# The low parts of the stick-breaking keys in both halves of the partitions

## The chip, the cores and the metric

The kernel runs on one core of one Trainium2 chip. A core has TensorE (in the profile PE for matmuls, PEld for its weight loads), VectorE (DVE), ScalarE (ACT), GpSimd (POOL) and a queue for transfers (SP). What counts is the time of one execution on the device in microseconds (us), as the median of several runs.

## The reference

The kernel computes two layers of a decoder trunk over 512 positions of width 1024. Layer 0 mixes with sliding-window attention and, beside it, stick-breaking attention of 8 heads with 64 channels; both layers end in cross-attention and a feed-forward network. Only the stick-breaking part is touched:

```
z = einsum('bqhd,bkhd->bhqk', q[:, t0:t1], k[:, :t1]) * (HEAD_DIM ** -0.5)
log_fail = where(causal, -softplus(z), 0.0)
log_after = cumsum(log_fail, axis=3, reverse=True) - log_fail
a = where(causal, exp(log_sigmoid(z) + log_after), 0.0)
out = einsum('bhqk,bkhd->bqhd', a, v[:, :t1])
```

Blocks of 128 queries see the keys up to their own block, so the four blocks of a head have scores of 128 x 128, 128 x 256, 128 x 384 and 128 x 512.

## The kernel before

All large products run as three matmuls on numbers that are split into a high part, rounded to the matmul's input format, and a low part, the rest: high by high, high by low, low by high (`mm3`, lines 182 to 184). They write the PSUM tile ps_pj, of which there are three buffers.

`sb_pair` handles two heads of 64 channels, which lie in the two halves of the 128 partitions of a query tile qb and a key tile kb_. For head `a`, `hr` is its own half and `orow` the other one. Three tiles are made of 128 x 512: `qs` holds the high part of the queries in `hr` (line 787, ScalarE) and their low part in `orow` (788, VectorE); `ks` holds the high part of the keys in `hr` (789, ScalarE) and the same numbers again in `orow` (790, ScalarE); `kl` holds the low part of the keys in `hr` alone (791, VectorE). The profile calls them sbqs, sbks and sbkl. Each has one buffer per `a`, so the next pair of heads writes where this one read.

For each block n the scores take two matmuls into ps_at (two buffers): line 798 over all 128 rows gives high queries by high keys plus low queries by high keys, line 799 over the 64 rows of `hr` adds high queries by low keys. There are 8 heads of 4 blocks, so 32 of each, 8 of each width. Two sigmoids follow on ScalarE (801, 804), which free the ps_at buffer, a masking of the diagonal on GpSimd (806, 808), a running product and a product on VectorE (811, 813), transposes on TensorE (821), a copy out by ScalarE (823) and the matmuls with the values (829), which use 64 columns of the array and write ps_ov.

Four calls of `sb_pair` are interleaved with work that is independent of them: the output projection of the sliding-window part (`out_proj`, with 512 columns), the preparation of the memory (`mem_prep`: transposes at line 332 into ps_pj, evacuated at 336 and 337) and the projection of the memory to keys and values (`mem_kv`, with 256 columns). Each weight tile is loaded, cast by ScalarE (170) and subtracted by VectorE (171). No order is written out by hand: a scheduler places all instructions by its own estimates of time, and each engine then runs its instructions strictly in the order it was given.

Of the kernel before, what the change touches and what calls it, by code (L numbers as in the profile page):

```python
# [33 lines left out]
def trunk(ctx, tc, x, mem, positions, norm_mix, norm_cross, norm_mem, norm_ffn,  # L34
# [5 lines left out]
    V, G, A, T, SY = nc.vector, nc.gpsimd, nc.scalar, nc.tensor, nc.sync  # L40
# [7 lines left out]
    def tl(pool, shape, tag, bufs=1, dt=FP32):  # L48
        return pool.tile(shape, dt, name=tag, tag=tag, bufs=bufs)
# [8 lines left out]
    def ps(tag, *shape):  # L58
        t = psp.tile([P, 512], FP32, name="ps_" + tag, tag="ps_" + tag, bufs=PSB[tag])
        if not shape:  # L60
            return t
        if len(shape) == 2:
            return t.rearrange("p (a b) -> p a b", b=shape[-1])[:, :shape[0]]
        return t[:, :shape[0]]

    def behind(ins, other):

        tc.add_manual_dep(ins.ins if hasattr(ins, "ins") else ins, (other.ins if hasattr(other, "ins") else other).name,
                          mybir.DependencyInfo(mybir.DependencyClass.NoSync, mybir.DependencyReason.DATA),
                          reason="side by side")  # L70

    def f32(ap):
        return ap.bitcast(FP32)
# [134 lines left out]
    def split(src, hi, lo, eng=None):  # L208
        A.copy(out=hi, in_=src)  # L209
        V.tensor_tensor(out=lo, in0=src, in1=f32(hi), op=ALU.subtract)  # L210
# [299 lines left out]
    def mixer0():  # L510
# [160 lines left out]
        for a in range(2):  # L671
            for g in range(2):
# [4 lines left out]
                             in_=sq.rearrange("p (t h d) -> p t h d", t=2, d=64), axis=AX.X)  # L677
# [101 lines left out]
        def sb_pair(c, qb, kb_):  # L779
            o = ps("ov")  # L780
            ats = []
            for a in range(2):
                hr = slice(64 * a, 64 * a + 64)

                orow = slice(64 - 64 * a, 128 - 64 * a)
                qs, ks, kl = (tl(bp, [P, S], f"{nm}{a}", 1, FP32R) for nm in ("sbqs", "sbks", "sbkl"))
                A.copy(out=qs[hr], in_=qb[hr])
                V.tensor_tensor(out=qs[orow], in0=qb[hr], in1=f32(qs[hr]), op=ALU.subtract)
                A.copy(out=ks[hr], in_=kb_[hr])
                A.copy(out=ks[orow], in_=f32(ks[hr]))  # L790
                V.tensor_tensor(out=kl[hr], in0=kb_[hr], in1=f32(ks[hr]), op=ALU.subtract)
                at = []
                ats.append(at)
                for n in range(NT):
                    wdt = (n + 1) * P
                    z = ps("at")
                    nq = slice(n * P, wdt)
                    T.matmul(z[:, :wdt], lhsT=qs[:, nq], rhs=ks[:, :wdt], start=True, stop=False)
                    T.matmul(z[:, :wdt], lhsT=qs[hr, nq], rhs=kl[hr, :wdt], start=False, stop=True)  # L799
                    be = tl(bp, [P, wdt], f"be{n}", 3 if n < 2 else 2)  # L800
                    A.activation(out=be[:, :wdt], in_=z[:, :wdt], func=AF.Sigmoid)
                    sn_ = tl(bp, [P, S + 1], "sbs", 2)
                    G.memset(sn_[:, wdt:wdt + 1], 1.0)
                    A.activation(out=sn_[:, :wdt], in_=z[:, :wdt], func=AF.Sigmoid, scale=-1.0)
                    dgs = slice(n * P, wdt)
                    G.affine_select(out=sn_[:, dgs], in_=sn_[:, dgs], pattern=[[-1, P]], compare_op=ALU.is_gt,
                                    fill=1.0, base=0, channel_multiplier=1)
                    G.affine_select(out=be[:, dgs], in_=be[:, dgs], pattern=[[-1, P]], compare_op=ALU.is_gt,
                                    fill=0.0, base=0, channel_multiplier=1)
                    ex_ = tl(bp, [P, S], "sbe", 2)  # L810
                    V.tensor_tensor_scan(out=ex_[:, wdt - 1::-1], data0=sn_[:, wdt:0:-1], data1=sn_[:, wdt:0:-1],
                                         initial=1.0, op0=ALU.mult, op1=ALU.bypass)
                    V.tensor_tensor(out=be[:, :wdt], in0=be[:, :wdt], in1=ex_[:, :wdt], op=ALU.mult)
                    at.append(be)

            for kb in range(NT):
                aTs = []
                for a in range(2):
                    pt = ps("tr", NT, P)
                    for n in range(kb, NT):  # L820
                        T.transpose(out=pt[:, n], in_=ats[a][n][:, kb * P:(kb + 1) * P], identity=ident)  # L821
                    aT = tl(bp, [P, NT, P], "sbaT", 2)
                    A.copy(out=aT[:, kb:], in_=pt[:, kb:])
                    aTs.append(aT)

                with tc.high_priority():
                    for a in (1, 0):
                        h = 2 * c + a
                        mm = T.matmul(o[64 * a:64 * a + 64, kb * P:], lhsT=vb[h // 4][:, kb, 64 * (h % 4):64 * (h % 4) + 64],  # L829
                                      rhs=aTs[a][:, kb:].rearrange("p a b -> p (a b)"), start=kb == 0, stop=kb == NT - 1)  # L830
                        if a:
                            first = mm
                        else:
                            behind(mm, first)
            hi, lo = tl(obp, [P, S], f"oh{c}", 1, FP32R), tl(obp, [P, S], f"ol{c}", 1, FP32R)
            split(o, hi, lo)
            oh[4 + c], ol[4 + c] = hi, lo
# [16 lines left out]

        qk_proj(0)
        sb_pair(0, *qks[0])
        sb_pair(1, *qks[1])
        qk_proj(1)
        sb_pair(2, *qks[2])
        sb_pair(3, *qks[3])  # L860

# [269 lines left out]
```

## Time and profile before

| | us |
|---|---|
| median of 3 runs | 1627.89 |
| lowest and highest | 1626.36, 1630.06 |
| the profiled execution | 1628.36 |
| its span, first to last instruction | 1626.6 |
| stick-breaking heads within it | about 150 to 278 |

The profile lists for each engine what it ran and when. A matmul's duration overlaps the next one's, so what a matmul costs in a dense stream is the distance between two starts. A weight load (PEld) of the next matmul can run beside the matmul before it. Idle time before an instruction is put down to what ended it.

### The profile page before, as it was taken

The page shows a single profiled execution, that of the slowest core. Times are in us where ns is not written, and L with a number is a line of the kernel's source. Part 1 is how long each engine was busy: PE and PEld are TensorE (multiplying, and loading weights), DVE is VectorE, ACT ScalarE, POOL GpSimd, SP SyncE. Part 2 cuts the span into 40 slices and gives each one's busy share as a digit, 9 for nine tenths or more (in the row PEclk, how much of TensorE's full clock was granted, in tenths as well). Part 3 has the DMA queues.
Part 4 walks back from the last instruction along what each step waited for, and adds up shares of the span by engine and source line. Part 5 has one row for each costly group of instructions (what it writes and reads, how often), then busy time and mean ns, then how long its engine had stood idle before and what let it go on. Part 6 is the DMA issues. An engine that isn't in the chain of part 4 may idle for free.

```text
span 1626.6 us, 21049 instructions
## 1 busy us (share of the span) xinstructions
PE 1604.9 (99%) x8298; PEld 1332.4 (82%) x8298; DVE 1017.4 (63%) x1662; ACT 706.7 (43%) x1246; POOL 200.9 (12%) x307
## 2 busy tenths in 40 slices
PE   7999999999999999999999999999999999999998
PEld 7987786888788888888789888998888788888887
DVE  6765785666675476366776677655555763674563
ACT  5565675554342243144434344443444441442341
POOL 4301332201100000000422123101002000000000
PEclk9999899999999999999999999999999999999999
DMA  6211331321323223222322222342203323323222
GB/s 191 79 53 63 111 102 61 111 78 52 103 78 104 91 90 104 80 95 74 114 79 59 75 76 78 126 159 79 78 27 104 104 78 104 98 83 104 86 76 72
DMA packets 144479, 145.57 MB, mean 89 GB/s; under 512 B 2844, under 2 KB 143837, under 8 KB 144381
## 3 DMA queue, kind: packets, MB, share of 16 engines
q1 hardware_dynamic: 143882, 143.98, 27.7%
q8 instruction: 66, 1.08, 0.3%
q0 software_dynamic: 96, 0.07, 0.1%
q14 instruction: 32, 0.26, 0.1%
q10 hardware_dynamic: 403, 0.18, 0.0%
HBM read 142.12 MB, written 2.10 MB: 89 GB/s over the span
## 4 chain that ended last, share of the span: by engine, by line
PE 97%; DVE 1%; ACT 1%; DMA 1%; issue 0%; SPq 0%; POOL 0%; DVEq 0%
PE ps_pj L182 28%; PE ps_pj L184 28%; PE ps_pj L183 28%; PE ps_at L953 1%; PE ps_ov L829 1%; PE ps_at L799 1%; DMA sbqk<-in_x_dram 1%; PE ps_tr L821 1%; PE ps_at L182 1%; PE ps_at L184 1%; PE ps_at L183 1%; PE ps_ov L985 0%; PE ps_at L933 0%; PE ps_tr L448 0%; PE ps_ov L750 0%; PE ps_ov L183 0%
## 5 line engine op out<-in xcount | busy, mean ns | idle before, releaser
L183 PE MATMUL ps_pj<-xl,whi 128*128 128x512 f32 x1088 | 432.4, 397 | 0.0
L182 PE MATMUL ps_pj<-xh,whi 128*128 128x512 f32 x1024 | 405.4, 397 | 2.0 <-DVE hF L1004 1.3
L184 PE MATMUL ps_pj<-xh,wlo 128*128 128x512 f32 x1024 | 407.2, 398 | 0.0
L170 ACT CAST whi<-wraw 128x1024 fp32r<-128x1024 f32 (+2 forms) x276 | 264.3, 1006 | 301.1 <-PE ps_pj L183 249.9
L171 DVE TENSOR_TENSOR wlo<-wraw,whi 128x1024 fp32r<-128x1024 f32 (+2 forms) x276 | 320.8, 1197 | 42.4 <-ACT whi L170 41.4
L183 PEld LDWEIGHTS ps_pj<-xl,whi 128*128 128x128 f32 x1088 | 204.4, 188 | 48.2 <-issue 0.7
L182 PEld LDWEIGHTS ps_pj<-xh,whi 128*128 128x128 f32 x1024 | 192.4, 188 | 47.5 <-DVE hF L1004 1.9
L184 PEld LDWEIGHTS ps_pj<-xh,wlo 128*128 128x128 f32 x1024 | 192.4, 188 | 45.4 <-issue 1.0
L281 DVE TENSOR_TENSOR xT<-ps_pj,xT 128x512 f32<-128x512 f32 x80 | 53.7, 687 | 152.5 <-PE ps_pj L184 152.5
L183 PE MATMUL ps_pj<-hid,whi 128*128 128x512 f32 x352 | 138.0, 397 | 0.0
L184 PE MATMUL ps_pj<-hid,wlo 128*128 128x512 f32 x352 | 137.8, 397 | 0.0
L182 PE MATMUL ps_pj<-hid,whi 128*128 128x512 f32 x352 | 137.3, 397 | 0.0
L184 PE MATMUL ps_pj<-whi,xl 128*128 128x256 f32 x416 | 120.1, 291 | 1.5 <-DVE xl L232 1.4
L472 DVE TENSOR_TENSOR fu<-ps_pj,rb 128x512 f32<-128x512 f32 x88 | 60.5, 692 | 90.1 <-PE ps_pj L184 90.0
L242 POOL TENSOR_TENSOR nacc<-nacc,nsq 128x512 f32<-128x512 f32 x36 | 52.5, 1457 | 507.1 <-ACT nsq L241 503.6
L183 PE MATMUL ps_pj<-ol,whi 128*128 128x512 f32 x256 | 101.8, 398 | 0.0
L184 PE MATMUL ps_pj<-oh,wlo 128*128 128x512 f32 x256 | 101.5, 398 | 0.0
L182 PE MATMUL ps_pj<-oh,whi 128*128 128x512 f32 x256 | 99.9, 403 | 1.1 <-ACT oh L209 1.1
L474 ACT ACTIVATE fa<-fu,ccol 128x512 f32<-128x512 f32 x88 | 71.3, 814 | 59.3 <-DVE fu L472 59.3
L182 PE MATMUL ps_pj<-whi,xh 128*128 128x256 f32 x288 | 82.4, 288 | 0.2 <-ACT xh L231 0.2
L183 PE MATMUL ps_pj<-wlo,xh 128*128 128x256 f32 x288 | 82.0, 287 | 0.0
L475 DVE SCALAR_TENSOR_TENSOR fa<-fu,ccol,fa 128x511 f32<-128x511 f32 x88 | 65.6, 748 | 25.8 <-ACT fa L474 25.8
(351 smaller groups left out, 2596.5 us busy)
## 6 DMA issues: line engine op xcount, KB each, us to landing
wraw<-in_ffn_w_up_dram SPq DMA_DIRECT2D x44, 1024.0 KB, 5.1
wraw<-in_xa_w_kv_dram SPq DMA_DIRECT2D x16, 1024.0 KB, 5.5
wraw<-in_ffn_w_down_dram SPq DMA_DIRECT2D x16, 1024.0 KB, 5.1
wraw<-in_hgrn_w_in_dram SPq DMA_DIRECT2D x16, 1024.0 KB, 5.6
wraw<-in_ab_w_in_dram SPq DMA_DIRECT2D x8, 1024.0 KB, 5.5
wraw<-in_xa_w_q_dram SPq DMA_DIRECT2D x8, 1024.0 KB, 5.2
wraw<-in_xa_w_o_dram SPq DMA_DIRECT2D x8, 1024.0 KB, 5.1
wraw<-in_ffn_w_down_dram SPq DMA_DIRECT2D x8, 768.0 KB, 4.9
```

The lines of the kernel that those rows point to most:

```text
L170: A.copy(out=hi[:, k, c], in_=raw[:, k, c])
L171: V.tensor_tensor(out=lo[:, k, c], in0=raw[:, k, c], in1=f32(hi[:, k, c]), op=ALU.subtract)
L182: T.matmul(o, lhsT=lh, rhs=rh, start=first, stop=False)
L183: T.matmul(o, lhsT=lh, rhs=rl, start=False, stop=False)
L184: T.matmul(o, lhsT=ll, rhs=rh, start=False, stop=last)
L242: (V if c == KC - 1 else G).tensor_tensor(out=self.acc, in0=self.acc, in1=sq, op=ALU.add)
L281: V.tensor_tensor(out=xT[m], in0=o, in1=xT[m], op=ALU.add)
L472: V.tensor_tensor(out=u, in0=o, in1=rb, op=ALU.mult)
L474: A.activation(out=a, in_=u, func=AF.Identity, scale=conv_col(l, 2, ch), bias=bias_col(l, ch))
L475: V.scalar_tensor_tensor(out=a[:, 1:], in0=u[:, :S - 1], scalar=conv_col(l, 1, ch), in1=a[:, 1:], op0=ALU.mult, op1=ALU.add)
L799: T.matmul(z[:, :wdt], lhsT=qs[hr, nq], rhs=kl[hr, :wdt], start=False, stop=True)
L821: T.transpose(out=pt[:, n], in_=ats[a][n][:, kb * P:(kb + 1) * P], identity=ident)
```

## The change

After line 791 ScalarE copies the low parts of the keys from `hr` to `orow`, once for each head, so that `kl` is filled in all 128 partitions. The second score matmul then takes all 128 rows of `qs` and `kl`. It so adds low queries by low keys, a term that was left out before. What stood at line 798 stands at 799 in the changed kernel, 799 at 800, and all later lines one further.

```
                 V.tensor_tensor(out=kl[hr], in0=kb_[hr], in1=f32(ks[hr]), op=ALU.subtract)
+                A.copy(out=kl[orow], in_=f32(kl[hr]))
...
                     T.matmul(z[:, :wdt], lhsT=qs[:, nq], rhs=ks[:, :wdt], start=True, stop=False)
-                    T.matmul(z[:, :wdt], lhsT=qs[hr, nq], rhs=kl[hr, :wdt], start=False, stop=True)
+                    T.matmul(z[:, :wdt], lhsT=qs[:, nq], rhs=kl[:, :wdt], start=False, stop=True)
```

The scheduler also orders some instructions of the stick-breaking stage differently; before it and after it the order is as it was, and the transfer queue's is unchanged throughout. On TensorE the first scores of the first head stood as follows, among projections (ps_pj) of the sliding-window output.

```order
L182 MATMUL ps_pj<-oh_915,whi 128x512
L183 MATMUL ps_pj<-ol_916,whi 128x512
L798 MATMUL ps_at<-sbks_1596,sbqs_1595 128x128
L799 MATMUL ps_at<-sbkl_1597,sbqs_1595 128x128
L798 MATMUL ps_at<-sbks_1596,sbqs_1595 128x256
L799 MATMUL ps_at<-sbkl_1597,sbqs_1595 128x256
L184 MATMUL ps_pj<-oh_915,wlo 128x512
```

In the changed kernel the same place reads so; the left-out rows are eight projections of 512 columns.

```order
L183 MATMUL ps_pj<-ol_916,whi 128x512
L799 MATMUL ps_at<-sbks_1596,sbqs_1595 128x128
L799 MATMUL ps_at<-sbks_1596,sbqs_1595 128x256
L184 MATMUL ps_pj<-oh_915,wlo 128x512
...
L184 MATMUL ps_pj<-oh_1236,wlo 128x512
L800 MATMUL ps_at<-sbkl_1597,sbqs_1595 128x128
L800 MATMUL ps_at<-sbkl_1597,sbqs_1595 128x256
L182 MATMUL ps_pj<-oh_915,whi 128x512
```

The two first matmuls are issued where they were, and ten projections stand between them and their second ones, which wait for the copied low parts.

On ScalarE this is the place in which the second block's scores of the third head (be, 128x256) follow the first block's; xl is the memory's prepared tile, whi a weight tile's high part.

```order
L336 ACTIVATE xl_2670<-ps_pj,gcol 128x256
L801 ACTIVATE be_1799<-ps_at 128x128
L804 ACTIVATE sbs<-ps_at 128x128
L170 CAST whi<-wraw 128x8x128 x2
L336 ACTIVATE xl_2692<-ps_pj,gcol 128x256
L801 ACTIVATE be_1814<-ps_at 128x256
L804 ACTIVATE sbs<-ps_at 128x256
```

In the changed kernel the copy (L792, here that of the fourth head) comes in between.

```order
L790 CAST sbks_1860<-sbks_1860 64x512
L802 ACTIVATE be_1802<-ps_at 128x128
L805 ACTIVATE sbs<-ps_at 128x128
L792 CAST sbkl_1861<-sbkl_1861 64x512
L170 CAST whi<-wraw 128x8x128 x2
L802 ACTIVATE be_1817<-ps_at 128x256
L805 ACTIVATE sbs<-ps_at 128x256
```

The copy stands ahead of the two weight casts. The L336 that stood between these casts and the next sigmoids now stands ahead of the copy of the keys' high parts (L790), as does the one before the first sigmoids here. Some way above, the two sigmoids of the second head's third block (128x384) stood ahead of the stage's first L336 and now stand behind it.

## Rows read from the trace of the kernel before

**Rows 1.** This is the page's first line and its part 1, TensorE's row: busy time, share of the span, instructions.

```profile
span 1626.6 us, 21049 instructions
PE 1604.9 (99%) x8298; PEld 1332.4 (82%) x8298; DVE 1017.4 (63%) x1662; ACT 706.7 (43%) x1246; POOL 200.9 (12%) x307
```

**Rows 2.** This is the page's part 4, the chain that ended last, by engine.

```profile
PE 97%; DVE 1%; ACT 1%; DMA 1%; issue 0%; SPq 0%; POOL 0%; DVEq 0%
```

**Rows 3.** This is busy time of each engine in four stretches (window in us, its length, then PE, PEld, DVE, ACT, POOL with counts of instructions, granted TensorE clock as a share of full speed, DMA share, GB/s). The stick-breaking heads run from 150 to 278 us.

```profile
150.00:172.00 22.00, 22.00 (x93) 16.11 (x91) 17.56 (x31) 14.91 (x33) 7.98 (x21) 1.00 0.40 128
172.00:190.00 18.00, 16.05 (x71) 10.55 (x70) 14.21 (x24) 13.49 (x29) 3.13 (x12) 0.72 0.51 165
190.00:265.00 75.00, 75.00 (x525) 62.10 (x524) 52.41 (x86) 49.88 (x116) 26.39 (x64) 1.00 0.27 85
265.00:278.00 13.00, 10.57 (x50) 5.61 (x50) 4.19 (x8) 4.49 (x10) 0.58 (x2) 1.00 0.02 6
```

**Rows 4.** This is the timeline of TensorE's matmuls around two pairs of score matmuls that stand between projections of 256 columns (start, duration, engine, line, out<-in, rows*columns of the array, shape). Durations overlap, so a step is read from start to start.

```profile
201.62 0.39 PE L798 MATMUL ps_at<-sbks,sbqs 128*128 128x512 f32 x1
201.94 0.50 PE L799 MATMUL ps_at<-sbkl,sbqs 64*128 64x512 f32 x1
202.36 0.39 PE L184 MATMUL ps_pj<-whi,xl 128*128 128x256 f32 x1
202.59 0.28 PE L182 MATMUL ps_pj<-whi,xl 128*128 128x256 f32 x1
202.71 0.28 PE L183 MATMUL ps_pj<-wlo,xl 128*128 128x256 f32 x1
...
203.06 0.22 PE L798 MATMUL ps_at<-sbks,sbqs 128*128 128x128 f32 x1
203.21 0.32 PE L799 MATMUL ps_at<-sbkl,sbqs 64*128 64x128 f32 x1
203.47 0.39 PE L183 MATMUL ps_pj<-wlo,xl 128*128 128x256 f32 x1
203.69 0.28 PE L184 MATMUL ps_pj<-whi,xl 128*128 128x256 f32 x1
```

**Rows 5.** This is the timeline of TensorE's weight loads around the first pair, whose matmuls start at 150.72 and 150.87; the same columns.

```profile
150.49 0.19 PEld L798 LDWEIGHTS ps_at<-sbks,sbqs 128*128 128x128 f32 x1
150.87 0.18 PEld L799 LDWEIGHTS ps_at<-sbkl,sbqs 64*128 64x128 f32 x1 [0.19 <-DVE xT L281]
...
151.75 0.19 PEld L184 LDWEIGHTS ps_pj<-oh,wlo 128*128 128x128 f32 x1
```

**Rows 6.** This is TensorE's timeline: two neighbouring projections of 512 columns, and transposes of 128 columns alone and four in a row (merged into one row that lasts from the first start to the last end).

```profile
158.84 0.40 PE L183 MATMUL ps_pj<-ol,whi 128*128 128x512 f32 x1
159.07 0.40 PE L184 MATMUL ps_pj<-oh,wlo 128*128 128x512 f32 x1
...
169.88 0.27 PE L821 MATMUL ps_tr<-ident,be 128*128 128x128 f32 x1
...
172.25 0.60 PE L332 MATMUL ps_pj<-ident,wraw 128*128 128x128 f32 x4
```

**Rows 7.** This is the instructions by line and shape, 130 to 300 us: count, busy us, mean ns of one, idle time before them.

```profile
L791 DVE TENSOR_TENSOR sbkl<-sbqk,sbks 64x512 fp32r<-64x512 f32 x8 | 5.4, 681 | 0.3
L790 ACT CAST sbks<-sbks 64x512 fp32r<-64x512 f32 x8 | 5.0, 620 | 0.2
...
L799 PE MATMUL ps_at<-sbkl,sbqs 64*128 64x512 f32 x8 | 4.3, 533 | 0.0
```

**Rows 8.** This is TensorE's timeline where it waits, in the stretch from 172 to 190 us; in brackets its idle time and what ended it.

```profile
175.59 0.38 PE L799 MATMUL ps_at<-sbkl,sbqs 64*128 64x256 f32 x1
177.78 0.62 PE L798 MATMUL ps_at<-sbks,sbqs 128*128 128x384 f32 x1 [1.81 <-ACT sbs L804]
...
180.58 0.80 PE L798 MATMUL ps_at<-sbks,sbqs 128*128 128x512 f32 x1
...
182.02 1.97 PE L829 MATMUL ps_ov<-sbaT,vb 128*64 128x512 f32 x4
```

**Rows 9.** This is ScalarE's timeline in the same stretch: the first row after an idle time, and two rows of the back-to-back work that follows it.

```profile
172.88 0.47 ACT L336 ACTIVATE xl<-ps_pj,gcol 128x256 fp32r<-128x256 f32 x1 [1.28 <-PE ps_pj L332]
...
177.60 2.00 ACT L170 CAST whi<-wraw 128x1024 fp32r<-128x1024 f32 x2
...
180.12 0.41 ACT L804 ACTIVATE sbs<-ps_at 128x256 f32<-128x256 f32 x1
```

**Rows 10.** This is busy time by stretch again, with the columns of rows 3, around the time in which the granted clock is low.

```profile
176.00:178.00 2.00, 0.22 (x1) 0.22 (x1) 1.94 (x3) 1.95 (x6) 0.47 (x3) 0.97 0.00 0
178.00:188.00 10.00, 9.86 (x32) 6.12 (x32) 8.48 (x16) 7.07 (x15) 1.14 (x5) 0.50 0.64 201
188.00:190.00 2.00, 2.00 (x15) 1.27 (x14) 0.46 (x1) 1.45 (x4) 0.58 (x2) 0.97 0.12 41
```

**Rows 11.** This is TensorE's timeline: the matmuls of the values (64 columns of the array) that directly follow an L799 matmul started at 212.67.

```profile
213.09 1.08 PE L829 MATMUL ps_ov<-sbaT,vb 128*64 128x512 f32 x4
```

**Rows 12.** This is ScalarE's timeline before the first scores.

```profile
150.21 1.14 ACT L170 CAST whi<-wraw 128x512 fp32r<-128x512 f32 x2 [1.74 <-PE ps_pj L183]
```

**Rows 13.** This is TensorE's timeline at the end of the last pair of heads: two of its waits.

```profile
269.07 0.33 PE L821 MATMUL ps_tr<-ident,be 128*128 128x128 f32 x1 [0.72 <-DVE be L813]
...
276.28 0.96 PE L182 MATMUL ps_pj<-oh,whi 128*128 128x512 f32 x3 [0.68 <-ACT oh L209]
```

## The prediction

> **What bounds the kernel now.** I read the page's shares first. TensorE is busy for 1604.9 of 1626.6 us [rows 1], and 97% of the chain that ended last runs on it [rows 2]. So a us taken from TensorE is a us of the kernel, wherever TensorE doesn't wait. Next I cut the stage that the change touches into stretches [rows 3]. From 150 to 172 and from 190 to 265 us TensorE never stops, and ScalarE and VectorE have spare time (in the long stretch 49.9 and 52.4 of 75 us). From 172 to 190 TensorE is busy for 16.05 of 18 us, at a mean granted clock of 0.72. There it has run out of projections and waits for ScalarE, 1.81 us for a buffer of scores [rows 8], while ScalarE runs back to back from 172.88 to 180.5 [rows 9]. From 265 to 278 the last heads end in a chain of small waits [rows 13]. Outside 150 to 278 us nothing is changed or moved.
>
> Then I looked at what a second score matmul costs, from start to start [rows 4]. Two neighbouring projections of 512 columns start 0.23 us apart [rows 6], two of 256 columns 0.12 (202.59 to 202.71) [rows 4]. The first score matmul of 512 columns takes 0.32 until the second starts, the second 0.42 until the next projection, and that projection, of 256 columns, 0.23. The weight loads show why [rows 5]: the load for L799 starts only at 150.87, with its own matmul, and the load after the next pair again only with its matmul at 151.75. In the dense stream the next load runs beside the matmul before. Something holds TensorE on the way into the 64-row matmul and on the way out of it.
>
> **Part 1, the second matmul on 128 rows.** It gets the form of its neighbours (128 rows, 128 columns, same input type, even the same stationary tile as the matmul before). No such second matmul is in the trace. Its lower bound is the projections' step, its upper bound what the 64-row form costs now. I take the lower one, since the row nearest in form is the projection.
> For 512 columns: now 0.32 + 0.42 + 0.23 = 0.97 us from the first score matmul to the second matmul behind the pair; then 0.23 + 0.23 + 0.12 = 0.58. That is 0.38 saved, with the decimals behind these figures. For 128 columns: now 0.15 + 0.26 + 0.22 = 0.63. A 128-column matmul can't follow faster than its weights: four transposes in a row take 0.60 against 0.27 for one, so (0.60 - 0.27) / 3 = 0.11 each [rows 6]. Then 0.11 + 0.11 + 0.12 = 0.34, so 0.29 saved. What is lost at the switches doesn't grow with the columns, and 256 and 384 columns take longer than a weight load, so I give them 0.38 too.
> With 8 pairs of each width [rows 7] the whole is 8 x 0.29 + 24 x 0.38 = 11.4 us of TensorE's time.
>
> **Where it counts.** Behind the stretch of waits lie the last five heads, 20 pairs: 5 x 0.29 + 15 x 0.38 = 7.15 us. By the new order two of these pairs directly precede the value matmuls (L829), which use 64 columns. There L829 starts 0.42 after L799 now [rows 11], and 0.42 - 0.23 = 0.19 of it may be L829's own switch and stay. That takes 0.4 off: **6.7 us**.
> Ahead of the stretch lie six pairs in the new order (two of 128 columns, two of 256, one of 384, one of 512): 0.6 + 1.5 = 2.1 us, and TensorE reaches the memory's transposes a further 0.6 us earlier because the second head's 384-column pair now stands among them. But there ScalarE sets the pace, so this gain is kept only as far as ScalarE also gets through sooner. It starts with the first L336, which the transposes release, so some 2.7 us earlier. Up to the sigmoid that frees the buffer at 180.5 it then has more to do: the two sigmoids of 384 columns that moved behind L336 (about 0.5 each, by the 0.47 to 0.60 of 256 and 512 columns) and one copy of 0.62. 2.7 - 1.0 - 0.6 = 1.1, so I count **1.2 us**, with what the five pairs in the stretch save besides.
>
> **Part 2, the copies on ScalarE.** Eight copies of 64 x 512, of the very form of L790, so 0.62 each [rows 7], 5.0 us in all. Apart from the one above they lie where ScalarE has a third of its time free [rows 3]. Behind each copy ScalarE's queue holds weight casts and sigmoids. The first two copies (1.24 us) stand ahead of a weight cast that waits 1.74 us for a buffer anyway [rows 12]: nothing. Each copy waits for L791 on VectorE (0.68), issued after the high part; where VectorE is late the copy could block ScalarE by up to that 0.68. I take 0, since other instructions stand between them in most heads and TensorE has work queued. If that cover is gone, 0.6 to 1.3 us per head.
>
> **Part 3, what is moved.** The first head's second matmuls stand ten projections later, as the changed order shows. They hold both score buffers for 10 x 0.23 = 2.3 us more. Nobody on TensorE needs these buffers meanwhile, and the sigmoids behind them start later against a ScalarE that has slack until 172. Nothing, except that work is handed into the stretch later; that is in the rivals. The transfers keep their order.
>
> **Sum.** 6.7 + 1.2 = 7.9 us. The profiled execution took 1628.4 us, so 1620.5; it lies 0.5 above the median, so I forecast a median of **1620.0 us** (0.49% less).
>
> **Rivals.**
> *All of it counts.* If the stretch of waits shrinks with the rest, the whole 11.4 less 0.4 is gained, and a shorter time at low clock adds to it. From 178 to 188 the clock is at 0.50, that is 1.2 GHz, after the wait of 1.81 us [rows 8, 10]; ten us at half speed hold up to 5 us of loss, of which perhaps 1.5 goes. That is up to 12.4 us: 1615.5 to 1617. Against it stands ScalarE's unbroken work there.
> *The stretch gets worse.* Scores handed in later, an added copy and two moved sigmoids let TensorE wait longer, and the low clock lasts longer: each 4 us more at half speed cost 2. The stretch then loses 1 to 5 us, and 6.7 becomes 2 to 6: 1622 to 1626.
> *Rows don't matter.* If the late weight loads come from the change of the moving tile or of the accumulating buffer, the change doesn't do what its form says: the delays stay, the copies are hidden, and the time is 1627 to 1629. Against it: projections also change their tile from one matmul to the next and show no delay, and the first score matmul, which changes the buffer too, has its weights loaded ahead [rows 5].
> The Trainium skill has a rule for this rival: the page "TensorE: Matmul & The Clock Gate", section "LDWEIGHTS", says that a weight load's time goes by its columns and that fewer rows make it no cheaper or dearer. By that rule alone the sum would be zero. The page "TensorEngine Tiling (Array Packing)", section "Key Properties", says that a change of tiling mode drains TensorE, which would give the sum above; the start-to-start rows speak for the second.
> *Slower: ScalarE's queue starves TensorE.* A copy that waits for VectorE holds up a weight cast, TensorE runs out of weights for some 2 us, and the clock falls as at 178: 2 us plus half of ten us, so 7 for each time. One such wait nearly cancels the gain, and from two on the kernel is slower: 1627.9 - 7.9 + 14 = 1634. For it: the stretch shows that one wait of 1.8 us was followed by low clock. Against it: from 190 to 265 TensorE has no idle time at all [rows 3].
>
> **Chances.** Forecast (gain of 6 to 10 us) 0.60; all of it counts 0.12; the stretch gets worse 0.13, two thirds of it beyond 0.2%; rows don't matter 0.10; slower 0.05. About 0.2%, 3.3 us, is what a measurement of this kernel can tell from no change. Faster: 0.60 + 0.12 + 0.09 = 0.81; the same: 0.04 + 0.10 = 0.14; slower 0.05. The range from 1615.5 to 1625.5 takes in the first two cases and most of the third, and leaves the last two out.
>
> **What would show it.** The weight load of the second score matmul starts beside the first, a good 0.1 us or more before its matmul; pairs of 512 columns take 0.23 + 0.23, with no 0.1 left on the next projection; eight new casts of 0.62 on ScalarE; the stretch from 190 to 265 shortened by 6 to 7 us; the first value matmuls (182.02 before) about 1 us earlier; one time at low clock of some ten us, and no second one. The prediction is wrong if L799's successor still loads its weights late, or if TensorE's idle time grows by more than 2 us.

## The result

| | median us | lowest to highest |
|---|---|---|
| before | 1628.97 (4 runs) | 1626.36 to 1630.49 |
| after | 1620.49 (4 runs) | 1620.13 to 1620.61 |

The ratio is 0.9949, with a 95% interval from 0.9932 to 0.9966: the changed kernel is 5.5 to 11 us faster. The runs of one kernel spread by some 4 us, the longer ones as a rule with the lower mean granted clock (among 25 of the kernel before, 1626.2 to 1626.9 us at 0.998 and 1630.1 to 1630.3 at 0.994), so the 8.5 us between these medians is itself uncertain; with 21 runs of before and 5 of after, further down, it is 7.2.

The page of the changed kernel answers to [rows 1]. TensorE's busy time fell by 10.7 us, from 1604.9 to 1594.2, while the span fell by 7.7. So its idle time grew by 3.0, from 21.7 to 24.7.

```profile
span 1618.9 us, 21062 instructions
PE 1594.2 (98%) x8298; PEld 1329.9 (82%) x8298; DVE 1017.4 (63%) x1662; ACT 711.2 (44%) x1254; POOL 204.0 (13%) x307
```

The timeline of TensorE's matmuls in the changed kernel, at two pairs between 256-column projections, answers to [rows 4] (start, duration, line, out<-in, array, shape).

```profile
198.34 0.39 PE L799 MATMUL ps_at<-sbks,sbqs 128*128 128x512 f32 x1
198.57 0.40 PE L800 MATMUL ps_at<-sbkl,sbqs 128*128 128x512 f32 x1
198.80 0.28 PE L184 MATMUL ps_pj<-whi,xl 128*128 128x256 f32 x1
198.92 0.28 PE L182 MATMUL ps_pj<-whi,xl 128*128 128x256 f32 x1
...
199.39 0.22 PE L799 MATMUL ps_at<-sbks,sbqs 128*128 128x128 f32 x1
199.45 0.28 PE L800 MATMUL ps_at<-sbkl,sbqs 128*128 128x128 f32 x1
199.56 0.33 PE L183 MATMUL ps_pj<-wlo,xl 128*128 128x256 f32 x1
199.73 0.28 PE L184 MATMUL ps_pj<-whi,xl 128*128 128x256 f32 x1
```

The 512-column pair takes 0.23 + 0.23 + 0.12 = 0.58 us where it took 0.97, and the 128-column pair 0.06 + 0.11 + 0.17 = 0.34 where it took 0.63. So one 128-column score matmul does follow the other after less than the 0.11 us of the transposes in a row [rows 6]; the next steps are as much longer.

The timeline of the weight loads, at the first head's second matmuls, answers to [rows 5].

```profile
153.92 0.19 PEld L184 LDWEIGHTS ps_pj<-oh,wlo 128*128 128x128 f32 x1
154.15 0.42 PEld L800 LDWEIGHTS ps_at<-sbkl,sbqs 128*128 128x128 f32 x2
154.50 0.19 PEld L182 LDWEIGHTS ps_pj<-oh,whi 128*128 128x128 f32 x1
```

The two L800 matmuls start at 154.38, so the first load runs 0.23 us ahead of them beside the projection, and the next projection's load starts at 154.50, 0.12 us ahead of its matmul at 154.62.

By stretch (window, length, PE, PEld, DVE, ACT, POOL, granted clock, DMA share, GB/s), as in [rows 3]:

```profile
150.00:172.00 22.00, 22.00 (x107) 18.04 (x106) 18.03 (x32) 15.86 (x36) 6.83 (x19) 1.00 0.38 120
172.00:190.00 18.00, 14.31 (x81) 9.64 (x80) 15.60 (x26) 14.91 (x32) 6.43 (x15) 0.81 0.54 175
190.00:265.00 75.00, 72.26 (x533) 61.83 (x533) 53.90 (x87) 54.03 (x123) 27.16 (x65) 1.00 0.27 85
265.00:278.00 13.00, 12.09 (x57) 8.14 (x54) 8.88 (x14) 8.60 (x17) 3.46 (x3) 1.00 0.30 90
```

From 172 to 190 TensorE now idles 3.7 us instead of 2.0, yet its mean clock is higher, 0.81 against 0.72. The last two windows can't be compared with those of before one by one, since all work has moved ahead.

TensorE's waits in the stretch of waits, from its timeline, answer to [rows 8].

```profile
174.42 0.39 PE L799 MATMUL ps_at<-sbks,sbqs 128*128 128x256 f32 x1 [0.96 <-ACT sbs L805]
...
175.50 0.42 PE L822 MATMUL ps_tr<-ident,be 128*128 128x128 f32 x1 [0.57 <-DVE be L814]
...
177.26 0.69 PE L799 MATMUL ps_at<-sbks,sbqs 128*128 128x384 f32 x1 [1.34 <-ACT sbs L805]
...
181.50 1.52 PE L830 MATMUL ps_ov<-sbaT,vb 128*64 128x512 f32 x4
```

There are more waits and they begin earlier, but the first value matmuls (L830, once L829) start sooner: 29.68 us behind the first score matmul (at 151.82), where it was 31.30 (from 150.72). The granted clock around them answers to [rows 10], with the columns of the stretches above.

```profile
174.00:176.00 2.00, 0.93 (x3) 0.44 (x3) 1.75 (x4) 1.95 (x5) 1.40 (x3) 0.90 0.76 258
176.00:182.00 6.00, 4.23 (x11) 2.20 (x13) 5.90 (x10) 5.95 (x14) 2.97 (x6) 0.50 0.07 15
182.00:184.00 2.00, 1.70 (x8) 0.52 (x5) 1.81 (x4) 1.79 (x4) 0.74 (x2) 0.89 0.94 314
```

The clock is at 0.50, that is 1.2 GHz, for 6.8 us (0.10 x 2 / 0.5 + 6 + 0.11 x 2 / 0.5), where it was for 10.2 before.

One wait is new, in the long stretch that had none.

```profile
207.86 0.39 PE L800 MATMUL ps_at<-sbkl,sbqs 128*128 128x512 f32 x1
209.25 0.41 PE L357 MATMUL ps_pj<-ident,kn 128*128 128x128 f32 x2 [1.00 <-DVE kn L372]
209.59 1.08 PE L830 MATMUL ps_ov<-sbaT,vb 128*64 128x512 f32 x4
```

The scheduler has put two transposes of the memory's keys (L357) ahead of the value matmuls. TensorE, now earlier there, waits 1.00 us for VectorE to make their input. In the order of before, all four stood behind the value matmuls.

To compare kernels I read marks from TensorE's timeline and count them from the first score matmul, since that start itself lies between 149.9 and 152.2 us in the ten profiles, with the same order of work on TensorE ahead of it. On ScalarE the first two copies come before it where they are made, and on VectorE two small instructions in the zeros kernel and a second subtraction in the kernel of the table's last row. The start doesn't follow these: without any of them it lies at 150.72 (before), 151.63 (last four heads) and 152.01 (two narrow matmuls). The kernels of the lower rows are explained in the next section. Four marks are the first memory transpose (L332), the first value matmul, the last block's first score matmul, and the first projection behind the last value matmul, which ends the stage.

| us from the first score matmul | first transpose | first value matmul | last score | end of stage |
|---|---|---|---|---|
| before | 21.53 | 31.30 | 114.01 | 125.56 |
| after | 18.43 | 29.68 | 105.46 | 116.90 |
| after, profiled again | 18.43 | 29.67 | 106.36 | 117.80 |
| order kept, 64 rows | 20.31 | 31.84 | 114.51 | 126.07 |
| zeros, no copies | 18.98 | 28.70 | 103.62 | 115.06 |
| copies only | 21.41 | 32.09 | 114.26 | 125.82 |
| two narrow matmuls | 22.72 | 34.12 | 116.31 | 127.87 |
| first four heads | 18.43 | 29.66 | 110.14 | 121.71 |
| last four heads | 21.53 | 31.31 | 108.37 | 119.81 |
| VectorE fills both halves | 18.96 | 29.05 | 104.77 | 116.21 |

The stage is 8.66 us shorter; the start was 1.10 later in the profile of after, and 0.1 was gained behind the stage, which gives its span of 7.7 less. In the second profile of after, with the same order, the stage is 7.76 shorter.

### The profile page after: what moved, and what is told of

It is laid out like the page before. It is cut to its first block, busy times and chain, and to the rows that moved or that the text cites. A ratio compares the mean times of both kernels' runs of the same rounds, so it can differ in the third digit from the quotient of the medians.

```text
span 1618.9 us, 21062 instructions
## 1 busy us (share of the span) xinstructions
PE 1594.2 (98%) x8298; PEld 1329.9 (82%) x8298; DVE 1017.4 (63%) x1662; ACT 711.2 (44%) x1254; POOL 204.0 (13%) x307
## 4 chain that ended last, share of the span: by engine, by line
PE 96%; DVE 1%; ACT 1%; DMA 1%; POOL 0%; issue 0%; SPq 0%; POOLq 0%; DVEq 0%
PE ps_pj L182 28%; PE ps_pj L183 28%; PE ps_pj L184 28%; PE ps_at L954 1%; PE ps_ov L830 1%; DMA wraw<-in_ab_w_in_dram 1%; PE ps_at L182 1%; PE ps_at L184 1%; PE ps_at L183 1%; PE ps_tr L822 0%; PE ps_ov L986 0%; PE ps_at L934 0%; PE ps_tr L448 0%; PE ps_ov L750 0%; PE ps_ov L183 0%; PE ps_ov L182 0%
## 5 line engine op out<-in xcount | busy, mean ns | idle before, releaser
L182 PE MATMUL ps_pj<-xh,whi 128*128 128x512 f32 x1024 | 406.9, 398 | 2.0 <-DVE hF L1005 1.3
L182 PEld LDWEIGHTS ps_pj<-xh,whi 128*128 128x128 f32 x1024 | 192.4, 188 | 47.8 <-DVE hF L1005 1.9
L182 PE MATMUL ps_pj<-hid,whi 128*128 128x512 f32 x352 | 137.3, 397 | 0.0
L182 PE MATMUL ps_pj<-oh,whi 128*128 128x512 f32 x256 | 99.5, 402 | 1.1 <-ACT oh L209 1.1
L182 PE MATMUL ps_pj<-whi,xh 128*128 128x256 f32 x288 | 83.1, 290 | 0.6 <-ACT xh L231 0.6
```

Of the source, the lines that this page charges most:

```text
L182: T.matmul(o, lhsT=lh, rhs=rh, start=first, stop=False)
```

## The experiments

The change does two things: it gives the second matmul 128 rows, and it adds copies, with a new order. The first two experiments take these apart. Each has on every engine the order of one of the two kernels, but for two instructions that the second adds on VectorE.

**The order and the copies of the changed kernel, with 64 rows.** Against the changed kernel:

```
-T.matmul(z[:, :wdt], lhsT=qs[:, nq], rhs=kl[:, :wdt], start=False, stop=True)
+T.matmul(z[:, :wdt], lhsT=qs[orow, nq], rhs=kl[orow, :wdt], start=False, stop=True)
```

> The changed kernel's instructions in the changed kernel's order on every engine, copies included, but the second score matmul reads 64 rows (the copied half of the low keys against the low queries, so the term of high queries by low keys is left out and the output is less exact). Theory (entering and leaving a 64-row matmul costs TensorE some 0.3 to 0.4 us a pair): the delays are back, 1628 to 1631 us, with 0.42 us from a 512-column second matmul to the next start. Rival (the scheduler's new order or the copies made the gain, rows don't matter): 1620 to 1622 us.

Measured: 1630.22 us, 1.0011 of before (1.0002 to 1.0020), where the changed kernel ran beside it at 1620.71. The delays are back as they were. First its timeline of matmuls, then that of its weight loads, around one pair:

```profile
202.71 0.39 PE L799 MATMUL ps_at<-sbks,sbqs 128*128 128x512 f32 x1
203.03 0.50 PE L800 MATMUL ps_at<-sbkl,sbqs 64*128 64x512 f32 x1
203.46 0.38 PE L184 MATMUL ps_pj<-whi,xl 128*128 128x256 f32 x1
```

```profile
203.03 0.18 PEld L800 LDWEIGHTS ps_at<-sbkl,sbqs 64*128 64x128 f32 x1 [0.24 <-issue]
203.46 0.19 PEld L184 LDWEIGHTS ps_pj<-whi,xl 128*128 128x128 f32 x1 [0.25 <-issue]
```

The loads are held back for 0.24 and 0.25 us on the way in and out, and no semaphore ends these times. With order and copies equal, the rows alone are worth 1630.2 - 1620.7 = 9.5 us. Within the stage it is 9.2 or 8.3 us, by which profile of after is taken. Of these, 1.7 or 0.8 arise between the first value matmul and the projections behind it, where no score pair stands and only the clock differs (low for 10.2 us with 64 rows, for 6.8 in both profiles of after); 7.5 remain by either, with L357's wait of 1.0 counted against them. Behind the stage the clock falls once more in the profile with 64 rows, which costs some 1.4 us. The rival that order or copies made the gain falls.

**The order of before, no copies, 128 rows.** The other half of the low keys is zero, so the sum is that of before. Against the kernel before:

```
+kls = [tl(bp, [P, S], f"sbkl{a}", 1, FP32R) for a in range(2)]
+for a in range(2):
+    orow = slice(64 - 64 * a, 128 - 64 * a)
+    V.tensor_scalar(out=kls[a][orow], in0=rb[orow], scalar1=0.0, scalar2=None, op0=ALU.mult)
...
+kl = kls[a]
...
-T.matmul(z[:, :wdt], lhsT=qs[hr, nq], rhs=kl[hr, :wdt], start=False, stop=True)
+T.matmul(z[:, :wdt], lhsT=qs[:, nq], rhs=kl[:, :wdt], start=False, stop=True)
```

> The order of the kernel before on every engine, no copies; the second score matmul takes all 128 rows, with the other half of the low keys set to zero once for all heads (two small instructions on VectorE). Theory: all the gain of the switches without the copies, 1618 to 1621 us; the stretch of waits should shorten by up to 1 us more than in the changed kernel, since ScalarE has no copies there. Rival (order or copies made the gain): 1627 to 1630 us.

Measured: 1616.89 us, 0.9932 (0.9920 to 0.9945). This beats both kernels, and by a us more than was expected; its slowest run (1618.81) lies below the changed kernel's fastest beside it (1619.07). The rows are worth 11.0 us here, 10.5 of it within the stage of the profile. Since the order is that of before, this can be followed matmul by matmul: 2.6 us are gained at the first value matmul, 4.0 at the projection (L182) that starts at 188.11 in the kernel before, and 10.5 at the end. No score pair stands between the first two of these points. The 1.4 us there come from the clock, which is full again 31.7 us behind the first score matmul here and 37.4 before. The remaining 6.5 are the last five heads. Its timeline has the same steps of 0.23 (its second matmul stands on line 805), and it waits in the stretch too, but gets to its value matmuls (L835) a us sooner than the changed kernel, counted from the first score:

```profile
197.01 0.39 PE L804 MATMUL ps_at<-sbks,sbqs 128*128 128x512 f32 x1
197.24 0.39 PE L805 MATMUL ps_at<-sbkl,sbqs 128*128 128x512 f32 x1
197.47 0.28 PE L184 MATMUL ps_pj<-whi,xl 128*128 128x256 f32 x1
```

```profile
175.56 0.44 PE L804 MATMUL ps_at<-sbks,sbqs 128*128 128x384 f32 x1 [1.86 <-ACT sbs L810]
...
179.74 1.98 PE L835 MATMUL ps_ov<-sbaT,vb 128*64 128x512 f32 x4
```

**The copies alone.** The copy is added to the kernel before, no matmul reads it. The order changes with it: L357 stands ahead of the value matmuls here too.

```
+A.copy(out=kl[orow], in_=f32(kl[hr]))
```

> The kernel before plus the eight copies on ScalarE, whose result no matmul reads; the second score matmul keeps its 64 rows. Theory (the copies are hidden but for one in the stretch of waits): 1628 to 1630 us, 0 to 1 us above the kernel before. Rival (the copies cost ScalarE's queue more): 1631 to 1636 us.

Measured: 1629.42 us, 1.0008 (1.0000 to 1.0017), so 0 to 2.8 us. The stage in its profile is only 0.26 longer: 0.79 us are lost at the first value matmul, behind one copy in the stretch of waits, and 0.5 come back later. Of the profiled difference of 2.3 us, 0.85 lies ahead of the first score matmul and 1.2 behind the stage, where the clock falls once more (columns of the stretches above).

```profile
278.00:282.00 4.00, 4.00 (x14) 3.09 (x13) 2.10 (x5) 1.48 (x3) 0.00 (x0) 0.64 0.06 16
```

**The changed kernel again**, as it is, beside these three.

> The changed kernel again, beside the others on the same chip: 1620.5 us, within 1 us.

Measured: 1620.71 us, 0.9954 (0.9941 to 0.9966).

**Two 64-row matmuls in a row.** Is the loss in each 64-row matmul, or in the change between forms? Against the kernel before:

```
-T.matmul(z[:, :wdt], lhsT=qs[hr, nq], rhs=kl[hr, :wdt], start=False, stop=True)
+for hc in (slice(0, wdt // 2), slice(wdt // 2, wdt)):
+    T.matmul(z[:, hc], lhsT=qs[hr, nq], rhs=kl[hr, hc], start=False, stop=hc.stop == wdt)
```

> The kernel before with each second score matmul cut into two 64-row matmuls of half the columns, one directly behind the other. Theory (the loss is in the change between 128 rows and 64, once in and once out): the second narrow one follows after its columns or a weight load, 0.06 to 0.2 us, and only the way in (0.1) and out (0.2 and 0.1) cost as before; 1627 to 1632 us. Rival (every 64-row matmul carries the loss, whatever stands beside it): another 0.3 us for each of 32, 1636 to 1638 us.

Measured: 1631.76 us, 1.0025 (1.0015 to 1.0035). First the matmuls (two alike are merged into one row), then the weight loads:

```profile
204.66 0.50 PE L800 MATMUL ps_at<-sbkl,sbqs 64*128 64x256 f32 x2
205.09 0.39 PE L183 MATMUL ps_pj<-wlo,xl 128*128 128x256 f32 x1
...
205.71 0.41 PE L800 MATMUL ps_at<-sbkl,sbqs 64*128 64x64 f32 x2
206.04 0.39 PE L183 MATMUL ps_pj<-wlo,xl 128*128 128x256 f32 x1
```

```profile
205.71 0.29 PEld L800 LDWEIGHTS ps_at<-sbkl,sbqs 64*128 64x128 f32 x2
206.04 0.19 PEld L183 LDWEIGHTS ps_pj<-wlo,xl 128*128 128x128 f32 x1
```

Two of 256 columns take 0.43 until the next projection, one of 512 took 0.42. Two of 64 take 0.33 where one of 128 took 0.26, and two weight loads stand there, 0.29 together. A 64-row matmul behind another one costs its columns or its weight load and nothing more. The loss belongs to the change of form, once in and once out. Of the 3.5 us above before, some 2.8 were already there at the first value matmul: its order in the stretch of waits is another one, and I did not follow that further.

**The change in some heads only**, by a condition on the call of `sb_pair` (c < 2 for the first four heads, c >= 2 for the last four):

```
+if c < 2:
+    A.copy(out=kl[orow], in_=f32(kl[hr]))
...
-T.matmul(z[:, :wdt], lhsT=qs[hr, nq], rhs=kl[hr, :wdt], start=False, stop=True)
+kr = slice(0, P) if c < 2 else hr
+T.matmul(z[:, :wdt], lhsT=qs[kr, nq], rhs=kl[kr, :wdt], start=False, stop=True)
```

> The change in the first four heads alone (copies and 128 rows); the last four keep 64 rows and have no copy. Theory: 16 pairs at some 0.36 us are given back, 1624 to 1626.5 us. Rival (ScalarE eats nearly all that is gained ahead of and in the stretch of waits, as the prediction had it): 1626.5 to 1628 us.

> The change in the last four heads alone. Theory: 16 pairs in the dense stretch give 16 x 0.36 = 5.7 us less four copies that cost little there, 1621.5 to 1623.5 us. Rival (the gain of the changed kernel comes mostly from a shorter time at low clock in the stretch of waits): 1625 to 1627 us.

Measured: 1624.29 us for the first four heads, 0.9978 (0.9969 to 0.9987), and 1624.79 for the last four, 0.9976 (0.9967 to 0.9985). In the stage they save 3.85 and 5.75 us, together 9.6, where the whole change saves 7.8 to 8.7 in two profiles. The 5.75 is what 16 pairs at 0.36 give, but by luck. Up to the first value matmul nothing is gained (31.31 and 31.30), and 1.25 us are gained at a projection that stands ahead of all changed pairs. The order of every engine is that of before until the clock is full again. First this projection's matmul before and here, then the stretch in which the clock is low here, with the one after it:

```profile
188.11 0.36 PE L182 MATMUL ps_pj<-whi,xl 128*128 128x256 f32 x1
...
187.78 0.36 PE L182 MATMUL ps_pj<-whi,xl 128*128 128x256 f32 x1
```

```profile
179.40:186.20 6.80, 6.36 (x19) 3.12 (x19) 6.77 (x13) 5.50 (x13) 0.97 (x4) 0.50 0.51 168
186.20:188.00 1.80, 1.80 (x17) 1.80 (x17) 1.24 (x3) 1.73 (x5) 0.00 (x0) 1.00 1.03 343
```

From the first score matmul (150.72 before, 151.63 here) that is 37.39 and 36.15. The clock is low for 6.8 us in the same work in which it was low for 10.2 before. The changed heads themselves gave 4.5 us. The median missed the expectation by 1.3 us, and a loss of that size stands behind the stage of the profile, where the clock falls.

```profile
272.00:276.00 4.00, 4.00 (x13) 3.12 (x12) 2.10 (x5) 1.43 (x3) 0.00 (x0) 0.63 0.06 16
```

That is (1 - 0.63) x 4 = 1.5 us by the mean clock. From the end of the stage to the end of the span it took 1351.6 us, against 1350.3 before.

**VectorE fills both halves**, by a second subtraction in place of ScalarE's copy:

```
-A.copy(out=kl[orow], in_=f32(kl[hr]))
+V.tensor_tensor(out=kl[orow], in0=kb_[hr], in1=f32(ks[hr]), op=ALU.subtract)
```

> The changed kernel's function, but VectorE subtracts a second time into the other half in place of ScalarE's copies, so the second half waits for no first. Theory (the copies cost 2 to 4 us through ScalarE's queue in and ahead of the stretch of waits): 1617 to 1619 us. Rival (any extra instruction of 0.6 us there costs the same, on VectorE as well): 1620 to 1622 us.

Measured: 1619.22 us, 0.9949 (0.9935 to 0.9963). The interval overlaps that of the changed kernel, and the runs (1618.06 to 1621.21 against 1619.07 to 1623.46) do so too. Its order is another one again, and its profile has the clock low for only 3.4 us. Whether the price of the copies is ScalarE's own or that of any extra 0.6 us there stays open.

## Why the prediction was right

The forecast of 1620.0 us was met by 1620.49, and a gain of 7.9 us by one of 8.5 (7.2 by the later runs). Its terms held unequally, and one of its own signs of being wrong came true: TensorE's idle time grew by more than 2 us, namely by 3.0. Of these 1.7 lie between 172 and 190 us and 1.0 at L357. The total held all the same.

**The price of the second matmul held exactly.** 0.58 and 0.34 us for the pairs were worked out from the neighbours' steps, and 0.58 and 0.34 were measured, for the 128 columns with another split of the steps. With order and copies held equal, the rows are worth 9.5 us, or 11.0 without copies, against the 11.4 - 0.4 that the prediction had for all 32 pairs; both hold differences in the time at low clock, and within the stage without them it is 7.5 (with L357's wait) and 9.1. The nearest test of the 6.7 us for the last five heads is the zeros kernel, with the order of before: 6.5.

**Rows matter: that rival is out.** Order and copies with 64 rows gave 1630 us. The Trainium skill's rule in "TensorE: Matmul & The Clock Gate", section "LDWEIGHTS", that a load's time goes by its columns, agrees with the bare durations (0.18 and 0.19 us); the cost lies in when the load starts. The Trainium skill's rule in "TensorEngine Tiling (Array Packing)", section "Key Properties", that a change of mode drains the engine, agrees with the held-back loads (0.24 and 0.25 us) and with two narrow matmuls in a row that pay once. The traces show the hold; they don't show what TensorE does in it.

**Ahead of and in the stretch: 1.2 us predicted, 1.6 measured** at the first value matmul (31.30 to 29.68). The steps were those forecast. The transposes came 3.1 us earlier and ScalarE's first L336 2.6 (2.7 predicted). Up to the end of the sigmoid that frees the buffer ScalarE took 8.92 us, where it had taken 7.65 [rows 9], so it gave back 1.3 (1.6 predicted, the two moved sigmoids and one copy).

```profile
171.37 0.48 ACT L336 ACTIVATE xl<-ps_pj,gcol 128x256 fp32r<-128x256 f32 x1
...
179.92 0.37 ACT L805 ACTIVATE sbs<-ps_at 128x256 f32<-128x256 f32 x1
```

The zeros kernel, which has neither, kept all: 2.55 at the transposes and 2.60 at the value matmuls.

**The long stretch: 6.7 us predicted, 6.9 measured** from the first value matmul to the last score (82.71 to 75.78), and 6.0 in the second profile of after. But two things lie in it that the prediction did not count. Before, TensorE still ran at 0.50 until 188 us, 3.6 us into the memory's projections that start at 184.48; in the first profile of after the clock is full when they start, which is worth 1.8, in the second it is low for 1.7 us more, and 0.9 is left. That the change did this isn't shown: with the last four heads alone the clock came back earlier too, with nothing changed ahead of it. Against it stands the new wait of 1.00 for L357. That leaves about 6.1 for the pairs by either profile.

**The copies and the order were mis-sized.** "Nothing" for seven copies and the moves was too low: the changed kernel's stage is 1.8 to 2.7 us longer than that of the zeros kernel, and its median 3.8 higher. One us of it lies in the stretch, which the prediction did price at 0.6 for the copy and 1.0 for the sigmoids, and one in L357's wait, which it did not see: the difference of order that it weighed was only that of the scores and of ScalarE. What the copies and the order cost one by one isn't taken apart. That the clock would fall once only held in the changed kernel's two profiles (between 150 and 300 us); that it would stay low for some ten us did not, it was 6.8.

**The other rivals.** The slower one did not come: no weight cast starved TensorE. TensorE did wait longer in the stretch, as the rival in which the stretch gets worse had it, but the low clock did not last longer. And the shorter low clock of the rival in which all of it counts was there, without its 1615.5 to 1617 us.

So the total was right in part by luck: two misses of 1 to 2 us, a shorter low clock and a new wait, stood against each other.

## What to carry to other kernels

Where a matmul on half the array's rows stands among full ones, look at the weight loads next to it: if they start with their matmul and not beside the one before, filling the idle rows with zeros can be cheaper than leaving them out (0.3 to 0.4 us a pair here, some 11 us in all). Fill them once and not by a copy for each use, if the values added are not needed. And when TensorE gets faster under a scheduler, read the new order for work that has been put ahead of what it need not precede.

## What was not expected of the hardware

The time at low clock was 10.2 us before and 6.8 after. It was 6.8 also with the change in the last four heads alone, whose work is that of before until the clock is full again. And in the kernel in which VectorE fills both halves the clock was back before 180 us:

```profile
176.00:180.00 4.00, 3.40 (x11) 1.73 (x11) 4.00 (x7) 3.54 (x9) 1.50 (x3) 0.57 0.13 28
180.00:184.00 4.00, 3.59 (x28) 2.82 (x26) 3.92 (x8) 2.78 (x7) 0.10 (x1) 1.00 1.03 339
```

More idle time of TensorE in that stretch did not mean a longer time at low clock. Nor did the same order mean the same time: counted from the first score matmul, the clock fell at 23.8 us in one profile of after and at 27.0 in the other, for 6.8 us in both, and the stage took 0.9 us longer in the second. In three of the ten profiles (copies only, order kept with 64 rows, last four heads) the clock also fell behind the last heads, and from the end of the stage to the end of the span these took 1351.5 to 1351.6 us. In seven it did not, and they took 1350.2 to 1350.4, with a like chain of waits of 2.4 to 2.7 us from the last score to the end of the stage in all ten. What decides between the two, I could not settle.
